# mLSTM's values ahead of stick breaking, and a start whose ACT and DVE order is written out

## The chip, the cores and the metric

The kernel runs on one core of one Trainium2 chip. The metric is the device time of one execution in microseconds (us), median of several runs; less is better. The engines of the core are TensorE (PE, matmuls), VectorE (DVE), ScalarE (ACT), GpSimd (POOL) and SyncE (SP, which starts most DMAs). Each engine runs its own list of instructions strictly in order; semaphores make one engine wait for another.

## The reference

Two layers of a hybrid block are applied to x (256 positions, width 1024), with 256 memory rows beside it. In each layer the normed x is projected to five branches of width 512 with 4 heads of 128, and to gates:

```
proj = rms_norm(x) @ w_in
y_sb = stick_breaking(sb_q, sb_k, sb_v)       # softplus, cumsum over keys, exp
y_ml = head_norm(mlstm(conv(ml_q), conv(ml_k), ml_v, i, f)) * sigmoid(ml_o)
y_gm = spatial_gating(gelu(gm_u), gelu(gm_v))
y_rt = head_norm(retention(rotary(rt_q), rotary(rt_k), rt_v))
y_xa = attention(xa_q, mem_k, mem_v)          # mem_k, mem_v = rms_norm(mem) @ w_mem_kv
merged = sum over branches b of sigmoid(gate_b) * ((y_b * silu(z_b)) @ w_up_b)
x = x + rms_norm(merged @ w_out)
```

Everything is fp32.

## The kernel before, in words

**Weights.** All weight matrices are cut into chunks of 128 x 2048, each of two halves of 128 x 1024, numbered in the order in which they are used (`CHUNKS`, from `SEQ_SECT`). SP loads a half into one of five `raw` buffers. ACT casts it to a rounded high part `whi` (L141), DVE subtracts to get the low part `wlo` (L142), and TensorE multiplies in three passes (high x high, low x high, high x low), which keeps fp32 accuracy. The input is kept in the same way as `hh` and `hl`. A half is 24 matmuls of 128 x 256 (`half_proj`, L216 to L218, output `psp`) or 12 of 128 x 512 (`half_nat`, L252 to L254, output `psn`), both eight blocks of the contraction, k0 to k7, by block order.

**A step.** `step(h)` splits half h+2, starts the load five halves on, issues the matmuls of half h, evacuates if a section ends, and pops a few units from `queue`. Units are the small pieces of the branches (scores, softplus, conv, gates, norms); so they lie between the halves.

**Order.** The whole program is traced in written order and then reordered by a scheduler with a model of the chip, engine by engine. Only inside `tc.manual_schedule(engines=...)` do the named engines keep the written order. In before this holds for SP in the prologue, for PE in the last matmuls of a layer and for SP, ACT, DVE and POOL in the tail.

**The prologue (layer 0).** The memory's keys (`mk`, halves 0 to 3) and values (`mv`, halves 4 to 7) are projected while x is loaded. Between them units do the memory's norm, the squares of x (L206), the product of x with its norm (`xr`, L378), the turning of x (`u2`, four times: four TensorE transposes into a PSUM tile `psh` that holds two blocks of x, then `hh` on ACT, L393, and `hl` on DVE, L394, block by block), and `rope_tables`: eight small DVE steps (`pf`, `ang`, `nn`) and then sin, abs and cos on ACT, which give `sinT` and `cosT`. mv is evacuated to a fp32 tile (L443) and split later by units (`mkv_split_units`, L449, L450). Half 8 is the first of `rt_q`, the first section of the layer, and needs `hh` and `hl`; half 12 is the first of `rt_v`.

**Stick breaking.** `sb_units` has three units for each of two head pairs g: `u1` (scores `psz`; abs, exp, ln on ACT, which are one softplus; a mask on POOL; high and low part `sh`, `sl`), `u2` (products of the triangle matrix with `sh` and `sl` into psz, exp to `sw`) and `u3` (values). Each change between exp and ln, and to tanh, needs a load of ACT's table. The units are popped during the section of mLSTM's values (`ml_v_section`, L725), which follows the four sb sections, and after it; `ml_gate_units` m1 to m4 (psc, psg, psm) are behind them.

Of the kernel before, what the change touches and what calls it, by code (L numbers as in the profile page):

```python
# [9 lines left out]
F32 = mybir.dt.float32  # L10
# [12 lines left out]
NSH = 1  # L23
# [8 lines left out]

SEQ_SECT = ["rt_q", "rt_v", "rt_k", "rt_z", "sb_q", "sb_k", "sb_v", "sb_z",
            "ml_v", "ml_q", "ml_k", "ml_z", "ml_o", "xa_q", "xa_z", "gm_u", "gm_v", "gm_z"]
BR = ["rt", "sb", "ml", "xa", "gm"]
# [48 lines left out]
def hybrid_kernel(ctx: ExitStack, tc: tile.TileContext, x, mem, wpl, wmv, pos, vec, row, post, gmw, cst, out):  # L84
# [325 lines left out]
    def mkv(l, units):  # L410
# [31 lines left out]
        def vevac(tb, ps):  # L442
            act.activation(mv[2][:, tb, :], ps, AF.Copy, scale=rcm[:, tb:tb + 1])  # L443
        nat(4, mh, ml, vevac, units)

    def mkv_split_units():

        def u(hi, lo, a):
            act.copy(hi, a)  # L449
            dve.tensor_tensor(lo, a, fview(hi), op=ALU.subtract)  # L450
        return [lambda m=m, s=s: u(*(a[:, s, :] for a in state[m]))
                for m, n in (("mk", 2), ("mv", 1)) for s in (slice(0, n), slice(n, 2 * n))]

    def layer(l):
# [84 lines left out]

        def sb_units():  # L540
            zp, sp, wt, po = {}, {}, {}, {}

            def part(tl, i):

                return (tl[:, 0:512] if i == 0 else tl[:, 512:768]).rearrange("p (h q) -> p h q", h=2)
# [7 lines left out]
            def u1(g):  # L553
                q, k = t["sb_q"], t["sb_k"]
                pss = [pz.tile([128, 2, 256 >> i], F32, tag="sm", name="psz") for i in range(2)]
                s = tp.tile([128, 768], F32, tag="sa", name="sa", bufs=2)
                hi = tp.tile([128, 768], F32R, tag="sh", name="sh", bufs=NSH)
                lo = tp.tile([128, 768], F32R, tag="sl", name="sl", bufs=NSH)
                for i in range(2):
                    for j in range(2):  # L560
                        h = 2 * g + j
                        pe.matmul(pss[i][:, j, :], k[:, h, i * 128:(i + 1) * 128], q[:, h, i * 128:T], start=j == 0,
                                  stop=False, skip_group_check=True)
                for i in range(2):
                    a = part(s[:], i)
                    act.activation(a, pss[i], AF.Abs)
                    act.activation(a, a, AF.Exp, scale=-1.0)
                    act.activation(a, a, AF.Ln, bias=1.0)
                    dve.scalar_tensor_tensor(a, pss[i], 0.0, a, op0=ALU.max, op1=ALU.add)
                mask(s[:])  # L570
                for c in (slice(0, 512), slice(512, 768)):
                    act.copy(hi[:, c], s[:, c])
                    dve.tensor_tensor(lo[:, c], s[:, c], fview(hi[:, c]), op=ALU.subtract)
                zp[g], sp[g] = pss, (hi, lo)

# [24 lines left out]

            return waves([[lambda g=g: u1(g), lambda g=g: u2(g), lambda g=g: u3(g)] for g in range(2)])

# [55 lines left out]
        def ml_gate_units():  # L658
            def m1():
                g = tp.tile([128, 2, 8], F32, tag="mg", name="mg", bufs=1)  # L660
                for tb in range(2):
                    dve.tensor_tensor(g[:, tb, :], psc["if"][tb], bif, op=ALU.add)
                f = g[:, :, 4:8]
                a = tp.tile([128, 2, 4], F32, tag="ma", name="ma", bufs=1)
                act.activation(a, f, AF.Abs)
                act.activation(a, a, AF.Exp, scale=-1.0)
                act.activation(a, a, AF.Ln, bias=1.0)
                lf = tp.tile([128, 2, 4], F32, tag="mlf", name="mlf", bufs=1)
                dve.scalar_tensor_tensor(lf, f, 0.0, a, op0=ALU.min, op1=ALU.subtract)
                t["g"], t["lf"] = g, lf  # L670

# [34 lines left out]

            return [m1, m2, m3, m4]

# [288 lines left out]
        queue.extend(mkv_split_units())  # L997
        nat(4, xh, xl, vcopy_to("rt_v"))
        section(proj, rope_to("rt_k"))
        nat(4, xh, xl, silu_nat("rt_z"))  # L1000
        drain()
        queue.extend(rt_units())
        section(proj, copy_to("sb_q", SCALE))
        section(proj, copy_to("sb_k"))
        nat(4, xh, xl, vcopy_to("sb_v"))
        section(proj, silu_to("sb_z"))
        drain()
        queue.extend(sb_units())
# [159 lines left out]
    with tc.manual_schedule(engines={mybir.EngineType.SP}):  # L1168
# [16 lines left out]
        for tb in range(2):  # L1185
# [114 lines left out]
```

## Time and profile before

| | |
|---|---|
| median of 3 runs | 919.64 us (919.44 to 919.68) |
| the profiled execution | 920.07 us |
| its span, first to last instruction | 918.2 us |
| mean granted TensorE clock | 0.998 |
| DVE busy | 603.7 us (66%) |
| ACT busy | 488.4 us (53%) |
| HBM read | 161.8 MB, 177 GB/s over the span |

The span is the profiled execution's stretch from its first to its last instruction; 1.9 us of the 920.07 lie around it. A matmul's record is longer than the distance to the next, since matmuls are pipelined: distances between starts tell what one costs. The granted clock is a share of TensorE's full speed of 2.4 GHz.

### The profile page before, as it was taken

The page shows a single profiled execution, that of the slowest core. Times are in us where ns is not written, and L with a number is a line of the kernel's source. Part 1 is how long each engine was busy: PE and PEld are TensorE (multiplying, and loading weights), DVE is VectorE, ACT ScalarE, POOL GpSimd, SP SyncE. Part 2 cuts the span into 40 slices and gives each one's busy share as a digit, 9 for nine tenths or more (in the row PEclk, how much of TensorE's full clock was granted, in tenths as well). Part 3 has the DMA queues.
Part 4 walks back from the last instruction along what each step waited for, and adds up shares of the span by engine and source line. Part 5 has one row for each costly group of instructions (what it writes and reads, how often), then busy time and mean ns, then how long its engine had stood idle before and what let it go on. Part 6 is the DMA issues. An engine that isn't in the chain of part 4 may idle for free.

```text
span 918.2 us, 13638 instructions
## 1 busy us (share of the span) xinstructions
PE 905.6 (99%) x5332; PEld 798.5 (87%) x5332; DVE 603.7 (66%) x882; ACT 488.4 (53%) x682; POOL 46.2 (5%) x66
## 2 busy tenths in 40 slices
PE   9999999999999999999999999999999999999997
PEld 7899999989998888888899999998999888888885
DVE  6776565776685665765588656559667765665555
ACT  6645459654665444455465444686556554444443
POOL 1000001000040000000010000010011300000000
PEclk9999999999999999999999999999999999999999
DMA  9665453554445545555556544435444545455551
GB/s 336 247 206 180 144 184 116 178 180 148 161 166 179 184 164 194 190 178 191 206 184 227 186 162 164 173 124 177 167 161 159 179 167 181 166 194 193 188 201 46
DMA packets 45857, 163.74 MB, mean 178 GB/s; under 512 B 5216, under 2 KB 5344, under 8 KB 45792
## 3 DMA queue, kind: packets, MB, share of 16 engines
q1 hardware_dynamic: 45072, 161.56, 49.8%
q10 hardware_dynamic: 720, 1.32, 0.4%
q8 instruction: 41, 0.67, 0.3%
q14 instruction: 24, 0.20, 0.1%
HBM read 161.80 MB, written 1.05 MB: 177 GB/s over the span
## 4 chain that ended last, share of the span: by engine, by line
PE 92%; ACT 2%; DMA 2%; issue 1%; DVE 1%; POOL 0%; ACTq 0%; DVEq 0%; POOLq 0%; SPq 0%
PE psn L252 17%; PE psn L253 17%; PE psn L254 17%; PE psp L218 9%; PE psp L217 9%; PE psp L216 9%; PE pout L1082 1%; PE pout L1084 1%; PE pout L1083 1%; DMA xn<-in_x_dram 1%; DMA memT<-in_mem_dram 1%; PE pss L766 1%; PE psx L877 1%; PE pso L911 1%; DVE wlo L142 1%
## 5 line engine op out<-in xcount | busy, mean ns | idle before, releaser
L142 DVE TENSOR_TENSOR wlo<-raw,whi 128x1024 fp32r<-128x1024 f32 (+1 forms) x293 | 359.8, 1230 | 229.7 <-ACT whi L141 228.7
L141 ACT CAST whi<-raw 128x1024 fp32r<-128x1024 f32 (+1 forms) x293 | 307.0, 1049 | 335.8 <-PE psn L254 185.1
L253 PE MATMUL psn<-wlo,hh 128*128 128x512 f32 x512 | 202.8, 396 | 0.0
L216 PE MATMUL psp<-hh,whi 128*128 128x256 f32 x704 | 200.5, 285 | 0.8 <-ACT whi L141 0.8
L254 PE MATMUL psn<-whi,hl 128*128 128x512 f32 x512 | 201.2, 393 | 0.0
L218 PE MATMUL psp<-hh,wlo 128*128 128x256 f32 x704 | 199.7, 284 | 0.5 <-DVE wlo L142 0.5
L217 PE MATMUL psp<-hl,whi 128*128 128x256 f32 x704 | 198.4, 282 | 0.0
L252 PE MATMUL psn<-whi,hh 128*128 128x512 f32 x512 | 185.9, 394 | 0.0
L216 PEld LDWEIGHTS psp<-hh,whi 128*128 128x128 f32 x704 | 133.1, 189 | 1.7 <-ACT whi L141 1.0
L218 PEld LDWEIGHTS psp<-hh,wlo 128*128 128x128 f32 x704 | 133.0, 189 | 1.0 <-DVE wlo L142 0.7
L217 PEld LDWEIGHTS psp<-hl,whi 128*128 128x128 f32 x704 | 132.9, 189 | 0.6
L254 PEld LDWEIGHTS psn<-whi,hl 128*128 128x128 f32 x512 | 96.2, 188 | 20.3
L253 PEld LDWEIGHTS psn<-wlo,hh 128*128 128x128 f32 x512 | 96.2, 188 | 20.1
L252 PEld LDWEIGHTS psn<-whi,hh 128*128 128x128 f32 x512 | 95.4, 188 | 20.9
L253 PE MATMUL psn<-wlo,yh 128*128 128x512 f32 x160 | 63.4, 396 | 0.0
L254 PE MATMUL psn<-whi,yl 128*128 128x512 f32 x160 | 62.6, 391 | 0.0
L252 PE MATMUL psn<-whi,yh 128*128 128x512 f32 x160 | 56.7, 393 | 0.0
L252 PEld LDWEIGHTS psn<-whi,yh 128*128 128x128 f32 x160 | 30.0, 188 | 6.9
L253 PEld LDWEIGHTS psn<-wlo,yh 128*128 128x128 f32 x160 | 30.1, 188 | 6.5
L254 PEld LDWEIGHTS psn<-whi,yl 128*128 128x128 f32 x160 | 30.1, 188 | 6.3
L1048 ACT ACTIVATE gate<-psn 128x512 f32<-128x512 f32 x40 | 24.0, 599 | 20.1 <-PE psn L254 20.1
L1083 PE MATMUL pout<-wlo,mgh 128*128 128x512 f32 x64 | 24.6, 395 | 0.0
(287 smaller groups left out, 1015.4 us busy)
## 6 DMA issues: line engine op xcount, KB each, us to landing
raw<-in_wpl_dram SPq DMA_DIRECT2D x290, 512.0 KB, 3.4
raw<-in_wmv_dram SPq DMA_DIRECT2D x4, 528.0 KB, 4.3
rowb<-in_row_dram SPq DMA_DIRECT2D x2, 772.0 KB, 7.3
raw<-in_wpl_dram SPq DMA_DIRECT2D x4, 256.0 KB, 6.2
xn<-in_x_dram SPq DMA_DIRECT2D x2, 512.0 KB, 7.6
gpost<-in_post_dram SPq DMA_DIRECT2D x2, 512.0 KB, 5.8
memT<-in_mem_dram ACTq DMA_DIRECT2D x3, 256.0 KB, 7.2
cs<-in_cst_dram SPq DMA_DIRECT2D x1, 768.0 KB, 7.1
```

The source lines that it names most:

```text
L141: act.copy(hi[:, c], r[:, c])
L142: dve.tensor_tensor(lo[:, c], r[:, c], fview(hi[:, c]), op=ALU.subtract)
L216: pe.matmul(ps_ap, wh(k), xh(k), start=st, stop=False, skip_group_check=True)
L217: pe.matmul(ps_ap, wh(k), xl(k), start=False, stop=False, skip_group_check=True)
L218: pe.matmul(ps_ap, wl(k), xh(k), start=False, stop=last and k == nk - 1, skip_group_check=True)
L252: pe.matmul(pss[tb], a, hi[:, c], start=k == 0, stop=False)
L253: pe.matmul(pss[tb], a, lo[:, c], start=False, stop=False)
L254: pe.matmul(pss[tb], b, hi[:, c], start=False, stop=k == 2 * nq - 1)
L766: pe.matmul(ps[:, 0:256], k[:, h, 0:128], q[:, h, :], start=True, stop=False, skip_group_check=True)
L877: pe.matmul(ps[:, tb, :], q[i], k[j], start=tb == 0 and i == j, stop=tb == 1 and i == 1, skip_group_check=True)
L1048: nat(4, xh, xl, lambda tb, ps: act.activation(gt[:, tb, :], ps, AF.Tanh, scale=0.5))
L1083: pe.matmul(po[tb][i], a, lo[:, c], start=False, stop=False)
```

## The change

1. `ml_v` moves ahead of the sb sections, in the order of chunks and in the program. Its matmuls, loads and splits go there.
2. `sb_units` takes the gate units as an argument. `u1` does both abs, both exp, both ln; the cast and subtract to `sh`, `sl` are a unit `us` of their own. The order becomes u1(0), u1(1) (with m0 and m1 of the gates inside it, split so that their exp and ln stand beside sb's), us(0), u2(0) with m2, us(1) with m3, u2(1) with m4, u3(0), u3(1).
3. mv is evacuated straight to its high part (ACT) and its low part (DVE, out of PSUM); the fp32 tile and two of four split units go.
4. From `mkv(0, ...)` until after rt_v of layer 0, ACT and DVE join SP in the manual region and keep the written order. The numbers of units popped in the prologue become 1, 2, 3, 2, 2, 1.
5. The first two of the four units that turn x stand ahead of `rope_tables`, the last two behind it.

```
-SEQ_SECT = ["rt_q", "rt_v", "rt_k", "rt_z", "sb_q", "sb_k", "sb_v", "sb_z",
-            "ml_v", "ml_q", "ml_k", "ml_z", "ml_o", "xa_q", "xa_z", "gm_u", "gm_v", "gm_z"]
+SEQ_SECT = ["rt_q", "rt_v", "rt_k", "rt_z", "ml_v", "sb_q", "sb_k", "sb_v", "sb_z",
+            "ml_q", "ml_k", "ml_z", "ml_o", "xa_q", "xa_z", "gm_u", "gm_v", "gm_z"]
...
         def vevac(tb, ps):
-            act.activation(mv[2][:, tb, :], ps, AF.Copy, scale=rcm[:, tb:tb + 1])
+            act.activation(mv[0][:, tb, :], ps, AF.Copy, scale=rcm[:, tb:tb + 1])
+            dve.scalar_tensor_tensor(mv[1][:, tb, :], ps, rcm[:, tb:tb + 1], fview(mv[0][:, tb, :]), op0=ALU.mult,
+                                     op1=ALU.subtract)
...
         return [lambda m=m, s=s: u(*(a[:, s, :] for a in state[m]))
-                for m, n in (("mk", 2), ("mv", 1)) for s in (slice(0, n), slice(n, 2 * n))]
+        return [lambda s=s: u(*(a[:, s, :] for a in state["mk"])) for s in (slice(0, 2), slice(2, 4))]
...
+                a = [part(s[:], i) for i in range(2)]
                 for i in range(2):
-                    a = part(s[:], i)
-                    act.activation(a, pss[i], AF.Abs)
-                    act.activation(a, a, AF.Exp, scale=-1.0)
-                    act.activation(a, a, AF.Ln, bias=1.0)
-                    dve.scalar_tensor_tensor(a, pss[i], 0.0, a, op0=ALU.max, op1=ALU.add)
+                    act.activation(a[i], pss[i], AF.Abs)
+                for i in range(2):
+                    act.activation(a[i], a[i], AF.Exp, scale=-1.0)
+                if g == 1:
+                    gate[0]()
+                for i in range(2):
+                    act.activation(a[i], a[i], AF.Ln, bias=1.0)
+                    dve.scalar_tensor_tensor(a[i], pss[i], 0.0, a[i], op0=ALU.max, op1=ALU.add)
+                if g == 1:
+                    gate[1]()
                 mask(s[:])
+                zp[g], sp[g] = pss, s
+
+            def us(g):
+                s = sp[g]
+                hi = tp.tile([128, 768], F32R, tag="sh", name="sh", bufs=NSH)
+                lo = tp.tile([128, 768], F32R, tag="sl", name="sl", bufs=NSH)
                 for c in (slice(0, 512), slice(512, 768)):
                     act.copy(hi[:, c], s[:, c])
                     dve.tensor_tensor(lo[:, c], s[:, c], fview(hi[:, c]), op=ALU.subtract)
-                zp[g], sp[g] = pss, (hi, lo)
+                sp[g] = hi, lo
...
-            return waves([[lambda g=g: u1(g), lambda g=g: u2(g), lambda g=g: u3(g)] for g in range(2)])
+            return [lambda: u1(0), lambda: u1(1), lambda: us(0), both(lambda: u2(0), gate[2]),
+                    both(lambda: us(1), gate[3]), both(lambda: u2(1), gate[4]), lambda: u3(0), lambda: u3(1)]
...
         nat(4, xh, xl, vcopy_to("rt_v"))
+        if l == 0:
+            state.pop("region").close()
...
         queue.extend(rt_units())
+        ml_v_section()
         section(proj, copy_to("sb_q", SCALE))
...
         drain()
-        queue.extend(sb_units())
-        ml_v_section()
-        queue.extend(ml_gate_units())
+        queue.extend(sb_units(ml_gate_units()))
...
-        queue.extend(xu[:2] + [mem_cols, lambda: [f() for f in state.pop("mk_evac")]] + xu[2:3] +
-                     [lambda: rope_tables(state.pop("pos"))] + xu[3:])
-        mkv(0, [1, 1, 2, 1, 3, 3])
+        queue.extend(xu[:2] + [mem_cols, lambda: [f() for f in state.pop("mk_evac")]] + xu[2:5] +
+                     [lambda: rope_tables(state.pop("pos"))] + xu[5:])
+        region = state["region"] = ExitStack()
+        E = mybir.EngineType
+        region.enter_context(tc.manual_schedule(engines={E.SP, E.Activation, E.DVE}))
+        mkv(0, [1, 2, 3, 2, 2, 1])
```

**The start on ACT.** First before, from the cast of half 5 (whi_215) to that of half 8 (whi_310):

```order
L141 CAST whi_215<-raw_175 128x1024 [waits DMAHW0_49]
L141 CAST whi_258<-raw_177 128x1024 [waits DMAHW1_49,DVE_49,PE_49]
L326 ACT_TABLE_LOAD
L326 ACTIVATE sinT_81<-ang_332 128x256 [waits DVE_49]
L199 COPY rbm_82<-psb_286 128x256 [waits PE_49]
L327 ACTIVATE ang_332<-ang_332 128x256 [waits Activation_49]
L141 CAST whi_290<-raw_213 128x1024 [waits DMAHW4_49]
L393 ACTIVATE hh_328<-psh_347,vecs_77 128x256 [waits DMAHW2_49,PE_49]
L330 ACTIVATE cosT_80<-ang_332,hp_344 128x256 [waits Activation_49]
L449 CAST mkh_152<-mk_156 128x512 [waits DVE_49] x2
L141 CAST whi_310<-raw_183 128x1024 [waits DMAHW2_49,PE_49]
```

The change, from the fourth block of hh to the two evacuations of mv; whi_331 is half 8, whi_375 half 9:

```order
L393 ACTIVATE hh_293<-psh_322,vecs_77 128x256 [waits DVE_49]
L141 CAST whi_331<-raw_184 128x1024 [waits DMAHW2_49,Activation_49]
L310 CAST tri_r_79<-cs_76 128x256
L326 ACT_TABLE_LOAD
L326 ACTIVATE sinT_81<-ang_351 128x256 [waits DVE_49]
L327 ACTIVATE ang_351<-ang_351 128x256 [waits Activation_49]
L330 ACTIVATE cosT_80<-ang_351,hp_363 128x256 [waits DVE_49,Activation_49]
L393 ACTIVATE hh_293<-psh_366,vecs_77 128x256 [waits PE_49]
L393 ACTIVATE hh_293<-psh_366,vecs_77 128x256 [waits DVE_49]
L141 CAST whi_375<-raw_191 128x1024 [waits DMAHW3_49,PE_49]
L442 ACTIVATE mvh_156<-psn_267,rcm_83 128x512 [waits PE_49,Pool_49]
L442 ACTIVATE mvh_156<-psn_268,rcm_83 128x512 [waits PE_49]
```

The sine table's load, sin and abs stood between the casts of halves 6 and 7, and cos behind the first hh; now all of them stand behind four blocks of hh and the cast of half 8, and ahead of the fifth block of hh.

**The start on DVE.** Before, from the first x product to the last step that gives ang and what follows it:

```order
L378 TENSOR_SCALAR xr_254<-xn_78,n0y_252 128x1024 [waits DMAHW5_49,Pool_49]
L314 TENSOR_SCALAR ang_332<-pf_330,cs_76 128x256 [waits DMAHW4_49,DVE_49]
L208 SCALAR_TENSOR_TENSOR rv_281<-ss_276 128x1 [waits Activation_49]
L192 TENSOR_SCALAR nv_210<-psn_207 128x2 [waits PE_49]
L317 TENSOR_SCALAR nn_333<-ang_332 128x256 [waits DVE_49]
L318 TENSOR_SCALAR nn_333<-nn_333 128x256 [waits DVE_49]
L378 TENSOR_SCALAR xr_254<-xn_78,n1y_283 128x1024 [waits DMAHW6_49,Pool_49]
L323 SCALAR_TENSOR_TENSOR ang_332<-nn_333,ang_332 128x256 [waits DVE_49]
L142 TENSOR_TENSOR wlo_216<-raw_175,whi_215 128x1024 [waits DMAHW0_49,Activation_49]
L323 SCALAR_TENSOR_TENSOR ang_332<-nn_333,ang_332 128x256 [waits DVE_49] x2
L142 TENSOR_TENSOR wlo_259<-raw_177,whi_258 128x1024 [waits DMAHW1_49,PE_49,Activation_49]
L325 TENSOR_SCALAR ang_332<-ang_332 128x256 [waits DVE_49]
```

The change, from the third and fourth block of hl to the first mv pass:

```order
L394 SCALAR_TENSOR_TENSOR hl_294<-psh_322,vecs_77,hh_293 128x256 [waits Activation_49] x2
L142 TENSOR_TENSOR wlo_332<-raw_184,whi_331 128x1024 [waits DMAHW2_49,DVE_49,Activation_49]
L313 CAST pf_349<-posb_120 128x256 [waits DMAHW7_49]
L314 TENSOR_SCALAR ang_351<-pf_349,cs_76 128x256 [waits DVE_49]
L317 TENSOR_SCALAR nn_352<-ang_351 128x256 [waits DVE_49]
L318 TENSOR_SCALAR nn_352<-nn_352 128x256 [waits DVE_49]
L323 SCALAR_TENSOR_TENSOR ang_351<-nn_352,ang_351 128x256 [waits DVE_49] x3
L325 TENSOR_SCALAR ang_351<-ang_351 128x256 [waits DVE_49]
L329 MEMSET hp_363 128x1
L394 SCALAR_TENSOR_TENSOR hl_294<-psh_366,vecs_77,hh_293 128x256 [waits Activation_49] x2
L142 TENSOR_TENSOR wlo_376<-raw_191,whi_375 128x1024 [waits DMAHW3_49,Activation_49]
L443 SCALAR_TENSOR_TENSOR mvl_157<-psn_267,rcm_83,mvh_156 128x512 [waits Activation_49]
```

The rotary steps stood between the x products and the subtracts of halves 5 and 6; now they stand in one piece behind the subtract of half 8 (wlo_332) and ahead of the last four blocks of hl.

**The first section on PE.** Before, from the fourth block of half 8 (whi_310, psp_410) on; psp_479 with whi_411 is half 10:

```order
L216 MATMUL psp_410<-hh_328,whi_310 128x256 [waits Activation_49]
L217 MATMUL psp_410<-hl_329,whi_310 128x256 [waits DVE_49]
L218 MATMUL psp_410<-hh_328,wlo_311 128x256
L216 MATMUL psp_479<-hh_328,whi_411 128x256 [waits Activation_49]
L217 MATMUL psp_479<-hl_329,whi_411 128x256
L216 MATMUL psp_410<-hh_328,whi_310 128x256 [waits Activation_49]
L218 MATMUL psp_479<-hh_328,wlo_412 128x256 [waits DVE_49]
L216 MATMUL psp_479<-hh_328,whi_411 128x256
L217 MATMUL psp_479<-hl_329,whi_411 128x256
```

The change, around the same blocks of half 8 (whi_331, psp_413):

```order
L216 MATMUL psp_413<-hh_293,whi_331 128x256
L217 MATMUL psp_413<-hl_294,whi_331 128x256
L218 MATMUL psp_413<-hh_293,wlo_332 128x256
L216 MATMUL psp_413<-hh_293,whi_331 128x256 [waits Activation_49]
L217 MATMUL psp_413<-hl_294,whi_331 128x256 [waits DVE_49]
L218 MATMUL psp_413<-hh_293,wlo_332 128x256
L216 MATMUL psp_413<-hh_293,whi_331 128x256 [waits Activation_49]
L217 MATMUL psp_413<-hl_294,whi_331 128x256 [waits DVE_49]
L218 MATMUL psp_413<-hh_293,wlo_332 128x256
```

Blocks of half 10 stood between the blocks of half 8; now half 8 is in the order of its blocks, with a wait for hh and one for hl at each of the last four.

**Stick breaking on ACT, layer 0.** Before, around u1 of the second head pair (sa_1532, sh_1533):

```order
L566 ACTIVATE sa_1532<-psz_1530 128x512 [waits PE_49,Activation_49]
L666 ACTIVATE ma_1717<-ma_1717 128x8 [waits Activation_49]
L567 ACTIVATE sa_1532<-sa_1532 128x512 [waits Activation_49]
L667 ACT_TABLE_LOAD
L667 ACTIVATE ma_1717<-ma_1717 128x8 [waits Activation_49]
L568 ACTIVATE sa_1532<-sa_1532 128x512 [waits Activation_49]
L566 ACTIVATE sa_1532<-psz_1531 128x256 [waits PE_49]
L141 CAST whi_1643<-raw_1407 128x1024 [waits DMAHW5_49,PE_49]
L567 ACT_TABLE_LOAD
L567 ACTIVATE sa_1532<-sa_1532 128x256 [waits Activation_49]
L572 CAST sh_1533<-sa_1532 128x512 [waits Pool_49]
L568 ACT_TABLE_LOAD
```

The change, u1 of the second pair (sa_1614) and the piece of the first that is still open (sa_1566, sh_1669):

```order
L564 ACTIVATE sa_1566<-psz_1565 128x256 [waits PE_49]
L566 ACTIVATE sa_1566<-sa_1566 128x256 [waits Activation_49]
L570 ACT_TABLE_LOAD
L570 ACTIVATE sa_1566<-sa_1566 128x256 [waits Activation_49]
L141 CAST whi_1639<-raw_1438 128x1024 [waits DMAHW6_49,DVE_49,PE_49]
L755 COPY ml_q_1531<-psp_1533 128x2x256 [waits PE_49]
L582 CAST sh_1669<-sa_1566 128x256 [waits Pool_49]
L564 ACTIVATE sa_1614<-psz_1612 128x512 [waits PE_49]
L564 ACTIVATE sa_1614<-psz_1613 128x256 [waits PE_49]
L566 ACT_TABLE_LOAD
L566 ACTIVATE sa_1614<-sa_1614 128x512 [waits Activation_49]
L566 ACTIVATE sa_1614<-sa_1614 128x256 [waits Activation_49]
```

ml_v's evacuations are gone from this place; the second pair's exp and ln stand in two blocks with one table load each, and its sh (sh_1758) follows later, behind two weight casts.

## Rows read from the trace of the kernel before

**Rows 1.** The page, part 1: busy us (share of the span) and instructions.

```profile
PE 905.6 (99%) x5332; PEld 798.5 (87%) x5332; DVE 603.7 (66%) x882; ACT 488.4 (53%) x682; POOL 46.2 (5%) x66
```

**Rows 2.** Waits of PE: line, waited for: us in total, times, longest.

```profile
PE psz L581 <- ACT sh L572: 3.0, 2, 1.5
```

**Rows 3.** Timeline of PE, 150 to 156.5 us: start, us, operation, idle before.

```profile
153.76 0.28 PE L216 MATMUL psp<-hh,whi 128*128 128x256 f32 x1
155.55 0.51 PE L581 MATMUL psz<-sh,tri_r 128*128 128x512 f32 x1 [1.51 <-ACT sh L572]
```

**Rows 4.** Timeline of PE, 31.5 to 37.2 us.

```profile
32.57 0.82 PE L389 MATMUL psh<-cs,xr 128*128 128x128 f32 x6
33.15 0.36 PE L216 MATMUL psp<-hh,whi 128*128 128x256 f32 x1
...
33.58 0.29 PE L216 MATMUL psp<-hh,whi 128*128 128x256 f32 x1
...
34.53 0.28 PE L218 MATMUL psp<-hh,wlo 128*128 128x256 f32 x1
35.63 0.39 PE L216 MATMUL psp<-hh,whi 128*128 128x256 f32 x1 [0.82 <-ACT whi L141]
```

**Rows 5.** Timeline of PE, 46.2 to 47.2 us.

```profile
46.65 0.63 PE L252 MATMUL psn<-whi,hh 128*128 128x512 f32 x2
```

**Rows 6.** Groups of ACT, 13 to 47 us: count, busy us, mean ns, idle before.

```profile
L141 ACT CAST whi<-raw 128x1024 fp32r<-128x1024 f32 x12 | 12.5, 1048 | 7.9 <-PE psp L217 5.6 <-DMA raw<-in_wpl_dram 2.3
...
L443 ACT ACTIVATE mv<-psn,rcm 128x512 f32<-128x512 f32 x2 | 1.4, 692 | 0.1
...
L330 ACT ACTIVATE cosT<-ang,hp 128x256 f32<-128x256 f32 x1 | 0.5, 506 | 0.0
```

**Rows 7.** Groups of DVE, 13 to 47 us.

```profile
L142 DVE TENSOR_TENSOR wlo<-raw,whi 128x1024 fp32r<-128x1024 f32 x10 | 12.2, 1222 | 3.9 <-ACT whi L141 3.9
L394 DVE SCALAR_TENSOR_TENSOR hl<-psh,vecs,hh 128x256 fp32r<-128x256 f32 x8 | 3.7, 477 | 0.5 <-ACT hh L393 0.5
...
L418 DVE TENSOR_TENSOR mk<-psk,rbm 128x512 f32<-128x512 f32 x2 | 1.3, 686 | 0.7 <-ACT rbm L199 0.7
...
L323 DVE SCALAR_TENSOR_TENSOR ang<-nn,ang 128x256 f32<-128x256 f32 x3 | 1.3, 421 | 0.0
```

**Rows 8.** Timeline of ACT, 13 to 39 us.

```profile
16.58 0.63 ACT L206 ACTIVATE sq<-xn 128x512 f32<-128x512 f32 x1 [0.76 <-DMA xn<-in_x_dram]
...
19.52 1.06 ACT L141 CAST whi<-raw 128x1024 fp32r<-128x1024 f32 x1 [0.30 <-DMA raw<-in_wpl_dram]
...
25.17 0.42 ACT L326 ACTIVATE sinT<-ang 128x256 f32<-128x256 f32 x1 [1.93 <-DVE ang L325]
...
33.07 0.47 ACT L393 ACTIVATE hh<-psh,vecs 128x256 fp32r<-128x256 f32 x1 [0.69 <-DVE hl L394]
```

**Rows 9.** Timeline of DVE, 17 to 28 us.

```profile
18.24 0.29 DVE L313 CAST pf<-posb 128x256 f32<-128x256 int32 x1
...
27.14 1.23 DVE L142 TENSOR_TENSOR wlo<-raw,whi 128x1024 fp32r<-128x1024 f32 x1
```

**Rows 10.** Stretches of 2 us: busy of PE, PEld, DVE, ACT, POOL, PEclk, DMA, GB/s.

```profile
912.00:914.00 2.00, 0.00 (x0) 0.00 (x0) 1.39 (x3) 0.51 (x2) 0.56 (x1) 1.00 0.38 148
914.00:916.00 2.00, 0.00 (x0) 0.00 (x0) 0.79 (x2) 0.00 (x0) 0.00 (x0) 0.51 0.48 185
```

**Rows 11.** Timeline of PE, 910.8 to 914 us.

```profile
911.33 0.40 PE L1084 MATMUL pout<-whi,mgl 128*128 128x512 f32 x1
```

**Rows 12.** Timeline of PE, 0 to 8 us.

```profile
1.34 4.63 PE L1175 MATMUL pw<-wm 128*128 128x256 f32 x10 [1.34 <-POOL wm L1172]
6.40 1.78 PE L296 MATMUL psk<-mg,raw 128*128 128x256 f32 x7 [0.43 <-DVE mg L350]
```

**Rows 13.** Timeline of ACT, 145 to 166 us.

```profile
150.03 1.28 ACT L667 ACT_TABLE_LOAD   x1
151.32 0.21 ACT L667 ACTIVATE ma<-ma 128x8 f32<-128x8 f32 x1
```

More of the change, by code (lines that the diff above doesn't have):

```diff
@@ L415, in mkv @@
         mk.append(bp.tile([128, H, T], F32, tag="gate", name="mk", bufs=2))
-        mv.append(bp.tile([128, 2, W], F32, tag="gate", name="mv", bufs=2))
         def evac(c, ps):
@@ L450, in u @@
             dve.tensor_tensor(lo, a, fview(hi), op=ALU.subtract)
-        return [lambda m=m, s=s: u(*(a[:, s, :] for a in state[m]))
-                for m, n in (("mk", 2), ("mv", 1)) for s in (slice(0, n), slice(n, 2 * n))]
+        return [lambda s=s: u(*(a[:, s, :] for a in state["mk"])) for s in (slice(0, 2), slice(2, 4))]
     def layer(l):
@@ L537, in diag, with sb_units @@
             return tl.rearrange("p (b q) -> p b q", b=3)[:, 0:3:2, :]
-        def sb_units():
+        def sb_units(gate):
             zp, sp, wt, po = {}, {}, {}, {}
@@ L556, in u1 @@
                 s = tp.tile([128, 768], F32, tag="sa", name="sa", bufs=2)
-                hi = tp.tile([128, 768], F32R, tag="sh", name="sh", bufs=NSH)
-                lo = tp.tile([128, 768], F32R, tag="sl", name="sl", bufs=NSH)
                 for i in range(2):
@@ L599, in u3, with both @@
                 y_from("sb", po, t["sb_z"], g)
-            return waves([[lambda g=g: u1(g), lambda g=g: u2(g), lambda g=g: u3(g)] for g in range(2)])
+            def both(*f):
+                return lambda: [u() for u in f]
+            return [lambda: u1(0), lambda: u1(1), lambda: us(0), both(lambda: u2(0), gate[2]),
+                    both(lambda: us(1), gate[3]), both(lambda: u2(1), gate[4]), lambda: u3(0), lambda: u3(1)]
         def waves(chains):
@@ L658, in ml_gate_units, with m0 @@
         def ml_gate_units():
-            def m1():
+            def m0():
                 g = tp.tile([128, 2, 8], F32, tag="mg", name="mg", bufs=1)
@@ L666, in m1 @@
                 act.activation(a, a, AF.Exp, scale=-1.0)
+                t["g"], t["ga"] = g, a
+            def m1():
+                g, a = t["g"], t["ga"]
+                f = g[:, :, 4:8]
                 act.activation(a, a, AF.Ln, bias=1.0)
@@ L669, in m1 @@
                 dve.scalar_tensor_tensor(lf, f, 0.0, a, op0=ALU.min, op1=ALU.subtract)
-                t["g"], t["lf"] = g, lf
+                t["lf"] = lf
             def m2():
@@ L705, in m4 @@
                 t["em"] = em
-            return [m1, m2, m3, m4]
+            return [m0, m1, m2, m3, m4]
         def ml_v_section():
```

## The prediction

> **What bounds the kernel now.** I read the page first: TensorE is busy for 905.6 of 918.2 us [rows 1], so only time in which it stands still, or runs at its lower clock, can be won or lost. The waits of PE say which those are: apart from the first microseconds the largest is psz behind sh, twice, 3.0 us in all [rows 2]. The timeline of PE around the first of them shows what one costs: the matmul ahead starts at 153.76 and psz at 155.55, where 0.12 is the usual distance, so 1.67 us, once in each layer, 3.3 us together [rows 3]. The other loss lies in the prologue. rt_q of layer 0 runs from 33.15 to the first psn of rt_v at 46.65, 13.5 us [rows 4, 5]; its 96 matmuls at the distance of [rows 4] (33.58 to 34.53, eight of them, 0.119 each) need 11.4, so 2.1 us are waits, the longest 0.82 for the cast of half 10. Nearly everything else is back to back. So the change is judged at two places: the two psz waits can give 3.3, rt_q's waits 2.1; all else can only cost.
>
> **The prologue, as now written.** ACT and DVE run what their order says, one after the other. Durations: cast 1.05, mv's evacuation 0.69, cos 0.51 [rows 6]; subtract 1.22, hl 0.48, a 128x512 pass out of PSUM 0.69, a rotary step on two tensors 0.42 [rows 7], one on a single tensor 0.29, by pf [rows 9]; hh 0.47, sin 0.42, and I take the same for abs, which has its shape [rows 8]. ACT overlaps two neighbours by some 0.1, a dependent step begins about 0.04 after its source.
>
> Early part: the squares of x, from 16.58 in before, now stand behind the cast of half 5, which waits for its DMA until 19.5 [rows 8]. They end some 3.6 later, and so do the x products on DVE. The cover is TensorE's work on mv, which lasts until 32.7; the first hh still comes at about 27.0, so I cost this at nothing. If the cover were gone it would cost up to 3.6.
>
> Turning x: hh of block k+1 waits for hl of block k where both lie in one PSUM tile; before shows it as hh with 0.69 idle behind hl [rows 8]. DVE had finished the subtract of half 7 at 27.14 + 1.23 = 28.4 [rows 9]; with the second x product and both mk products ahead of it I take 28.7. From there hl0, hh1, hl1, hl2, hh3, hl3 follow as a chain to 31.6. The cast of half 8 stands behind hh3 on ACT (to 32.0), its subtract behind hl3 on DVE (to 33.3).
>
> Then the rotary tables. Before started them at 18.24 in the gaps of DVE, and sin ran at 25.17 [rows 8, 9]. Now all eight DVE steps stand behind the subtract of half 8: five of 0.29 and three of 0.42 with 0.04 between are 3.0 us, to 36.2. ACT has loaded the sine table by then and waits: sin, abs, cos, to 37.7. Queued behind cos on ACT is hh of k4, and behind that everything: hh4 is there at 38.05.
>
> TensorE is ahead of this. It issues the last mv matmul and reaches rt_q at 32.7 (the last six transposes, from 32.57 in before [rows 4], now lie earlier), waits 0.34 for the subtract of half 8, and has done k0 to k3 at 34.5. In the new PE order half 8 runs strictly from k0 to k7, where before put half 10's first blocks in between. So it waits 3.6 for hh4. Then k4 and k5 cost 1.07 (hl4, hh5, hl5, one after the other). Ahead of hh6 ACT does the cast of half 9 and both mv evacuations (to 41.2), so hh6 costs 1.74; ahead of hl6 DVE does that half's subtract and the two new mv passes (to 42.5), so hl6 costs 1.21; hh7 and hl7 0.67. Sum 0.34 + 3.60 + 1.07 + 1.74 + 1.21 + 0.67 = 8.6. rt_v starts at 32.7 + 11.4 + 8.6 = 52.7 in place of 46.65 [rows 5]: **+6.1 us**. TensorE has no slack later to give it back.
>
> **The clock.** After the last matmul (911.33, 0.40 long) the granted clock is 0.51 in the stretch 914 to 916: it went from 2.4 to 1.2 GHz some 2.3 us after that matmul ended [rows 10, 11]. The wait for hh4 has 3.3 us without a matmul, and the next 5 us have few. At the program's start the ten pw matmuls, 0.46 apart, take 4.63 us, and the same kind runs 0.25 apart from 6.40 [rows 12], so some 4.6 us of work pass at the lower clock before it rises, which costs half of them. Here the dense work resumes at 43.9. I add **2.3**; ends 0 (no fall, or full speed again by 44) and 4.0 (full speed only with rt_v, at 52: half of the 8 us from 44). The Trainium skill, page "TensorE: Matmul & The Clock Gate", Part 1, calls the throttled clock the default to which an idle engine returns; by it the 2.3 is paid, and the row at the end agrees.
>
> **Values straight from PSUM.** mv's fp32 tile and its two split units go: two casts and two subtracts less, two DVE passes out of PSUM more, which I price by mk's 0.69 [rows 7]. They are counted above. No DMA is added; the weight loads keep their number, ml_v's chunks stand earlier on SP's queue because the section does. That queue runs five halves ahead throughout (five raw buffers), so the move costs nothing; without that cover TensorE would stand for what a load is late.
>
> **The stick-breaking stage, per layer.** Before put ml_v between sb_z and ml_q, and the sh of the second head pair came 1.67 after TensorE wanted it. Now u1(0) starts inside sb_z, us(0) is a unit of its own, and u2(0) stands 72 matmuls (8.6 us) and four psz behind the last psz of pair 0, while ACT needs about 6 us for what lies ahead of sh (abs, exp, a table load, ln, a cast, one copy, sh). u2(1) stands 96 matmuls behind its psz, 11.4 us and the psz besides, against about 10 on ACT. So both waits go: **-3.3**. What is late next is psc: its PSUM buffer is free only when ACT has read sw, and by the same walk that comes within 0.1 of TensorE's arrival; 0 taken, 0.5 a layer as the upper end. The cast of the last sb_z half, behind ACT's abs, load, exp, load, ln of pair 0, has 0.65 to spare: no cost, up to 0.5 a layer. ACT's table loads go from 6 to 8 a layer here; at 1.28 each and with the next ACTIVATE 0.01 behind [rows 13] they lie in the walk. The Trainium skill, page "ScalarE: Activation LUTs", section "What ACT_TABLE_LOAD costs", adds a drain of about 1.38 us to every switch. By that page the three loads ahead of psc would make it 4.1 later in each layer and the sum 933 (an estimate from its figure); [rows 13] show no drain.
>
> **Sum.** The profiled execution took 920.07 (span 918.2), 0.43 above the runs' median of 919.64. 920.07 + 6.1 + 2.3 - 3.3 = 925.2; on the runs' scale **924.7**.
>
> **The rivals.**
> *The clock holds.* 922.4. For it: the only fall that the trace shows is one, at the end, and half 8's few matmuls break up the idle time. Against it: 3.3 us without any matmul is more than the 2.3 after which it fell. Chance 0.20.
> *The stage gains less or nothing.* If the two extra loads and the cast ahead of sb_z put waits of 0.5 to 1.7 a layer in place of the old, the time is 925.7 to 928. For it: the margins of 0.1 and 0.65. Chance 0.09.
> *Each table switch holds ACT longer than its load.* If it were twice the 1.28, the three loads between u1(1) and psc would bring psc 3.8 late in each layer: 924.7 + 7.7 = 932.4. Against it: the next ACTIVATE starts 0.01 behind the load [rows 13]. Chance 0.01.
> *Faster: the start's chain is shorter than the stage's gain.* One mechanism: the chain hl0 to hl7, with the rotary steps in it. If it ends before 40.8 instead of 43.9, rt_v starts less than 3.1 us late, the wait for hh4 is too short for the clock, and the 3.3 of the two stages win; with the chain hidden altogether (rt_v at 46.65) it is 919.64 - 3.3 = 916.3, with rt_q's 2.1 gone too 914.2. For it: the stage's gain is sure by comparison. Against it: eight DVE steps, three on ACT and the two mv passes must then lie elsewhere, and the written order leaves them no other place. Chance 0.08.
> *The change does not do what it says* (the start's order is as free as before): 916.3 as well; the new order of both engines says otherwise, 0.02 within the last.
>
> **How the numbers follow.** Forecast 924.7, chance 0.62 with its own range 923.5 to 926.5; the clock case 0.20, the stage case 0.09, the table case 0.01, the faster case 0.08. About 0.2%, or 1.8 us, is what a measurement of this kernel can tell from no change, so the same is 917.8 to 921.5. Faster by more: 0.06, most of the last case. Same: 0.08, the rest of it and the lower part of the clock case with a start that loses 1 less. Slower: 0.86. The range leaves out the faster case and the worst of the stage case: 921.2 to 927.0.
>
> **What would show it.** In the profile after: rt_v's first psn near 52.7; a PE wait of over 3 us for hh near 34.6, led by ACT's cos; psp behind hl and hh a few times more before 44; a granted clock below 1 somewhere from 36 to 48, and matmuls of 128x256 more than 0.2 apart there; no psz behind sh in either layer; eight table loads there. The prediction is wrong if rt_v starts before 50, if the order of half 8's blocks on PE hides hh4, or if PE shows new waits over 1 us at psc or at sb_z's last half.

## The result, and the profile after

The changed kernel takes 925.16 us (median of 4 runs, 924.10 to 925.97), before 919.66 (4 runs); the ratio is 1.0055, 95% interval 1.004 to 1.007. It is slower, by 5.5 us, where 924.7 was forecast. The profiled execution took 924.86 with a span of 923.1, 4.9 more than before's 918.2, and a mean granted clock of 0.992.

The waits of PE, line and what was waited for, us in total, times, longest. The two psz waits of [rows 2] are gone; hh and hl have come:

```profile
PE psp L216 <- ACT hh L393: 4.5, 2, 3.3
PE pw L1195 <- POOL wm L1192: 1.3, 1, 1.3
PE psp L217 <- DVE hl L394: 0.9, 1, 0.9
```

The timeline of PE around rt_q, the counterpart of [rows 4, 5] (start, us, operation, idle before):

```profile
33.59 0.28 PE L216 MATMUL psp<-hh,whi 128*128 128x256 f32 x1
...
34.92 0.28 PE L218 MATMUL psp<-hh,wlo 128*128 128x256 f32 x1
38.51 0.58 PE L216 MATMUL psp<-hh,whi 128*128 128x256 f32 x1 [3.30 <-ACT hh L393]
...
42.00 0.58 PE L216 MATMUL psp<-hh,whi 128*128 128x256 f32 x1 [1.15 <-ACT hh L393]
43.44 0.58 PE L217 MATMUL psp<-hl,whi 128*128 128x256 f32 x1 [0.86 <-DVE hl L394]
...
48.04 0.40 PE L218 MATMUL psp<-hh,wlo 128*128 128x256 f32 x1
...
48.40 0.28 PE L217 MATMUL psp<-hl,whi 128*128 128x256 f32 x1
...
55.06 0.63 PE L252 MATMUL psn<-whi,hh 128*128 128x512 f32 x2
```

rt_q starts at 33.59 and rt_v at 55.06, where before had 33.15 and 46.65: 8.4 us late. The last matmul of block k3 stands at 34.92, the first of k4 at 38.51; k6 waits again for its hh (42.00) and its hl (43.44). The timeline of ACT in the same stretch:

```profile
36.69 0.42 ACT L326 ACTIVATE sinT<-ang 128x256 f32<-128x256 f32 x1 [2.64 <-DVE hp L329]
37.14 0.42 ACT L327 ACTIVATE ang<-ang 128x256 f32<-128x256 f32 x1
37.58 0.51 ACT L330 ACTIVATE cosT<-ang,hp 128x256 f32<-128x256 f32 x1
38.00 0.46 ACT L393 ACTIVATE hh<-psh,vecs 128x256 fp32r<-128x256 f32 x1
...
40.31 1.27 ACT L442 ACTIVATE mvh<-psn,rcm 128x512 fp32r<-128x512 f32 x2
41.46 0.48 ACT L393 ACTIVATE hh<-psh,vecs 128x256 fp32r<-128x256 f32 x1
```

And the timeline of DVE:

```profile
24.97 0.75 DVE L378 TENSOR_SCALAR xr<-xn,n1y 128x1024 f32<-128x1024 f32 x1 [0.66 <-POOL n1y L102]
...
27.97 1.22 DVE L142 TENSOR_TENSOR wlo<-raw,whi 128x1024 fp32r<-128x1024 f32 x1
29.11 0.47 DVE L394 SCALAR_TENSOR_TENSOR hl<-psh,vecs,hh 128x256 fp32r<-128x256 f32 x1
...
32.48 1.23 DVE L142 TENSOR_TENSOR wlo<-raw,whi 128x1024 fp32r<-128x1024 f32 x1 [0.45 <-ACT whi L141]
33.62 0.29 DVE L313 CAST pf<-posb 128x256 f32<-128x256 int32 x1
...
36.36 0.29 DVE L325 TENSOR_SCALAR ang<-ang 128x256 f32<-128x256 f32 x1
...
41.59 1.40 DVE L443 SCALAR_TENSOR_TENSOR mvl<-psn,rcm,mvh 128x512 fp32r<-128x512 f32 x2
42.91 0.47 DVE L394 SCALAR_TENSOR_TENSOR hl<-psh,vecs,hh 128x256 fp32r<-128x256 f32 x1
```

The second x product starts at 24.97, the subtract of half 7 at 27.97, and the first hl, with which the chain of hh and hl begins, at 29.11. The subtract of half 8 starts at 32.48, the first rotary step at 33.62, the last at 36.36; ACT has been idle for 2.64 when sin starts at 36.69; then come cos and, at 38.00, hh of k4. Behind that mv's two evacuations stand ahead of hh of k6 on ACT (40.31, 41.46), mv's two passes ahead of its hl on DVE (41.59, 42.91).

The stretches of 2 us (busy of PE, PEld, DVE, ACT, POOL, then PEclk, DMA share, GB/s):

```profile
36.00:38.00 2.00, 0.00 (x0) 0.00 (x0) 0.62 (x3) 1.25 (x4) 0.00 (x0) 1.00 0.18 70
38.00:40.00 2.00, 1.49 (x4) 1.08 (x4) 0.97 (x2) 1.45 (x4) 0.00 (x0) 0.51 0.00 0
...
46.00:48.00 2.00, 2.00 (x11) 2.00 (x11) 1.31 (x2) 0.12 (x1) 0.00 (x0) 0.50 0.99 404
48.00:50.00 2.00, 2.00 (x18) 2.00 (x17) 0.44 (x1) 0.52 (x1) 0.00 (x0) 0.93 0.96 350
```

From 38 to 48 the granted clock is 0.50, which is 1.2 GHz; up to 48.04 the matmuls start 0.21 apart, from 48.40 on 0.12. TensorE started no matmul between 34.92 and 38.51.

Later, the stage. The group of PE from 130 to 180 us that waited in before:

```profile
L591 PE MATMUL psz<-sh,tri_r 128*128 128x512 f32 x2 | 0.8, 390 | 0.0
```

And the timeline of ACT at the first pair's exp and ln:

```profile
142.82 1.28 ACT L566 ACT_TABLE_LOAD   x1
144.11 0.63 ACT L566 ACTIVATE sa<-sa 128x512 f32<-128x512 f32 x1
144.76 1.28 ACT L570 ACT_TABLE_LOAD   x1
146.06 0.63 ACT L570 ACTIVATE sa<-sa 128x512 f32<-128x512 f32 x1
```

psz behind sh no longer has any idle time ahead of it, against 1.5 in before [rows 3]. Each table load of 1.28 is followed by its ACTIVATE 0.01 to 0.02 later, as in [rows 13].

Not everything in this stage stands where the program writes it, since the scheduler orders ACT freely there. The gates' m0 and m1, written inside u1(1), run at 103.90 and 105.44 with a table load of their own between them. And not every change to or from tanh takes a load: behind the load for tanh at 149.52 an exp at 156.67 runs without one.

The account: rt_v is 8.41 later, the two psz waits (1.67 and, in layer 1, 1.65) are 3.32 less, which makes 5.09; the last matmul starts 4.94 later than in before [rows 11]:

```profile
916.27 0.40 PE L1104 MATMUL pout<-whi,mgl 128*128 128x512 f32 x1
```

### The profile page after: what moved, and what is told of

Read it like the earlier page. It is cut to its first block, busy times and chain, and to the rows that moved or that the text cites. A ratio compares the mean times of both kernels' runs of the same rounds, so it can differ in the third digit from the quotient of the medians.

```text
span 923.1 us, 13648 instructions
## 1 busy us (share of the span) xinstructions
PE 909.8 (99%) x5332; PEld 802.3 (87%) x5332; DVE 606.6 (66%) x882; ACT 488.6 (53%) x678; POOL 45.5 (5%) x66
## 3 DMA queue, kind: packets, MB, share of 16 engines
q10 hardware_dynamic: 720, 1.32, 0.4%
## 4 chain that ended last, share of the span: by engine, by line
PE 95%; DVE 2%; DMA 1%; issue 1%; ACT 1%; DVEq 0%; POOLq 0%; POOL 0%; ACTq 0%
PE psn L252 17%; PE psn L253 17%; PE psn L254 17%; PE psp L217 9%; PE psp L216 9%; PE psp L218 9%; PE pout L1102 1%; PE pout L1104 1%; PE pout L1103 1%; DMA raw<-in_wpl_dram 1%; PE psk L296 1%; PE pss L785 1%; PE psx L896 1%; PE pso L930 1%; PE psz L560 1%
## 5 line engine op out<-in xcount | busy, mean ns | idle before, releaser
L142 DVE TENSOR_TENSOR wlo<-raw,whi 128x1024 fp32r<-128x1024 f32 x293 | 360.1, 1232 | 231.6 <-ACT whi L141 230.4
L141 ACT CAST whi<-raw 128x1024 fp32r<-128x1024 f32 x293 | 306.6, 1048 | 335.0 <-PE psn L254 187.3
L216 PE MATMUL psp<-hh,whi 128*128 128x256 f32 x704 | 202.6, 288 | 4.5 <-ACT hh L393 4.5
```

The source lines that it names most:

```text
L141: act.copy(hi[:, c], r[:, c])
L142: dve.tensor_tensor(lo[:, c], r[:, c], fview(hi[:, c]), op=ALU.subtract)
L216: pe.matmul(ps_ap, wh(k), xh(k), start=st, stop=False, skip_group_check=True)
```

## The experiments

Nine kernels were run, one of them twice: four on one chip, then three on a second and three on a third, each group beside before (919.66, 919.70 and 919.84 us). The theory is the prediction's: the start loses through the rotary tables' place and mv's evacuation ahead of hh, the low clock comes on top, and the stage gains its two waits.

### e1: the stage alone

Parts 1 and 2 of the change, on before's prologue:

```
-        queue.extend(... + xu[2:5] + [lambda: rope_tables(state.pop("pos"))] + xu[5:])
-        region.enter_context(tc.manual_schedule(engines={E.SP, E.Activation, E.DVE}))
-        mkv(0, [1, 2, 3, 2, 2, 1])
+        queue.extend(... + xu[2:3] + [lambda: rope_tables(state.pop("pos"))] + xu[3:])
+        mkv(0, [1, 1, 2, 1, 3, 3])
```

and mv's evacuation and split as in before.

> The change's parts 1 and 2 alone (ml_v ahead of stick breaking, the units of stick breaking and of the gates in their new order); the prologue and the evacuation of mv are those of before. My theory: the two psz waits of 1.67 go, nothing comes in their place, so 919.66 - 3.3 = 916.3 us. Rival that the start's delay itself made room in the later stages: the psz waits come back or psc waits, 917.5 or more. Rival that the new order also loses elsewhere: 919 or more.

916.43 us, ratio 0.9964 (0.9949 to 0.9978): 3.2 less than before. The waits of PE hold no psz and no psc; what is left behind the first microseconds are rt_q's two:

```profile
PE psp L216 <- ACT whi L141: 1.0, 1, 1.0
PE psp L218 <- DVE wlo L142: 0.5, 1, 0.5
```

The gain does not hang on the start's delay, and the new order of the stage takes nothing back.

### e2: the start alone

Parts 3 to 5 on before's stages (the reverse of e1's edit).

> Parts 3 to 5 alone (mv straight from PSUM, ACT and DVE in written order until after rt_v, x turned ahead of the rotary tables); the stages from rt_k on are those of before. My theory: rt_v starts 8.4 later than in before, as in the changed kernel, and both psz waits stay: 919.66 + 8.4 = 928.1 us. Rival that part of the 8.4 is given back later: below 926.5.

928.84 us, ratio 1.010 (1.0085 to 1.0115): 9.2 more than before. Both groups of waits stand side by side:

```profile
PE psp L216 <- ACT hh L393: 4.4, 2, 3.3
PE psz L581 <- ACT sh L572: 3.0, 2, 1.5
```

e1's 3.2 less and e2's 9.2 more make 5.9, the changed kernel has 5.5 more: the parts add up, within the spread of the runs. In e2's profile rt_v starts at 54.48 and the last matmul at 919.16, both 7.83 later than in before: nothing of the start's loss is given back later. The profiled execution is 8.7 longer than before's, so some 0.8 of that lies behind the last matmul, where the change does nothing; why, no run shows.

### e3: the changed kernel with a free order

```
-        E = mybir.EngineType
-        region.enter_context(tc.manual_schedule(engines={E.SP, E.Activation, E.DVE}))
         mkv(0, [1, 2, 3, 2, 2, 1])
```

> The changed kernel, but ACT and DVE are free to be reordered in the prologue, as in before; units, the place of the rotary tables in the program and mv's evacuation are the change's. Theory that the written order is what costs: the rotary steps lie early again, rt_v starts at 46 to 46.7, the time is 915.0 to 916.3 us. Rival that turning x ahead of the rotary tables, or the new pop numbers, cost by themselves: rt_v at 50 or later, 920 us or more.

915.47 us, ratio 0.9953 (0.9938 to 0.9968); run again as e10 it took 915.71. The scheduler puts the rotary steps where before had them, though the program writes them behind the turns of x. Its timeline of DVE, the first and the last of the steps:

```profile
18.59 0.29 DVE L313 CAST pf<-posb 128x256 f32<-128x256 int32 x1 [0.95 <-DMA posb<-in_pos_dram]
...
24.67 0.29 DVE L325 TENSOR_SCALAR ang<-ang 128x256 f32<-128x256 f32 x1
```

Its timeline of PE, the start of rt_q, its one wait and the start of rt_v:

```profile
32.96 0.36 PE L216 MATMUL psp<-hh,whi 128*128 128x256 f32 x1
...
36.14 0.39 PE L218 MATMUL psp<-hh,wlo 128*128 128x256 f32 x1 [0.82 <-DVE wlo L142]
...
45.55 0.63 PE L252 MATMUL psn<-whi,hh 128*128 128x512 f32 x2
```

pf at 18.59, the last step at 24.67, and rt_v at 45.55, 9.5 us ahead of the changed kernel, with one wait of 0.82 in rt_q. So neither the pop numbers nor the written place of the rotary tables cost anything while the order is free; holding ACT and DVE to what is written does. Which piece of it costs what, e5 and e6 show.

### e4: TensorE's long waits filled

Half 8 gets 45 more matmuls into a tile that nobody reads:

```
+                if k == 6:
+                    dummy(6, 8)
...
+                if k in (3, 5):
+                    dummy(k, 27 if k == 3 else 10)
```

> The changed kernel with 45 more matmuls of 128x256 in half 8 of rt_q, into a PSUM tile that nobody reads: 27 behind k3, 10 in k5 and 8 in k6, each lot shorter than TensorE's wait there. Theory that the lower clock from 38 to 48 is a cost of its own, of 2.4 us: the clock stays at 1.00, the waits for hh and hl keep their ends (38.5, 42.0, 43.4), rt_v starts at 52.7 and the time is 922.7 us. Rival that the low clock is covered by the waits: the time stays at 925.2. Rival that the filler delays the blocks behind it: 926 or more.

922.92 us, ratio 1.0031 (1.0018 to 1.0044): 2.24 less than the changed kernel, with 45 matmuls more. Its stretches of 2 us, and the start of rt_v on PE:

```profile
38.00:40.00 2.00, 1.86 (x11) 1.46 (x12) 1.01 (x3) 1.53 (x3) 0.00 (x0) 1.00 0.00 0
...
46.00:48.00 2.00, 2.00 (x19) 2.00 (x19) 1.35 (x3) 0.74 (x1) 0.00 (x0) 1.00 1.04 408
```

```profile
52.84 0.63 PE L271 MATMUL psn<-whi,hh 128*128 128x512 f32 x2
```

The clock stays at 1.00 and rt_v starts at 52.84 in place of 55.06. rt_q itself started at 33.04, 0.55 earlier than in the changed kernel's profile, so of the 2.22 some 1.7 are the clock's in this pair of profiles. The lower clock is a cost of its own; the rest of the start's loss stays in e4.

### e5: the rotary tables written early

The written order stays; the eight DVE steps go, in pieces, ahead of the memory norm and around the two x products, and sin, abs and cos ahead of the first hh:

```
+        ra, rb, rc, rd = rope_units(state.pop("pos"))
+        queue.insert(0, ra)
+        xu = x_norm_units(0, (rb, rc))
+        queue.extend(xu[:2] + [mem_cols, lambda: [f() for f in state.pop("mk_evac")]] + xu[2:3] + [rd] + xu[3:])
...
+        mkv(0, [2, 2, 3, 3, 1, 1])
```

> The changed kernel, ACT and DVE still in written order, with the rotary tables written early: the DVE steps in four pieces ahead of the memory norm's column and around the two x products, sin, abs and cos behind the cast of half 7 and ahead of the first hh. Everything else is the change's. Theory that the place of the rotary tables is what costs most, and not that the order is written: the wait for hh4 goes, the clock stays at 1.00, the waits for hh6, hl6 and hl7 behind mv's evacuation stay (about 3.4 in all): 918.7 us. Rival that any written order costs what this one does, since the hh and hl pairs follow one another: 923 or more.

921.66 us (919.87 to 922.54, 11 runs), ratio 1.0019 (1.001 to 1.0028): 3.5 better than the changed kernel, 3.0 worse than expected. The wait for hh of k4 is gone, as expected. Two things were missed. In its profile cos waits for a fill of 0.06 us on DVE that was written behind the subtract of half 7 (timelines of ACT and, below, of DVE):

```profile
29.41 0.51 ACT L341 ACTIVATE cosT<-ang,hp 128x256 f32<-128x256 f32 x1 [1.29 <-DVE hp L340]
```

```profile
28.07 1.22 DVE L142 TENSOR_TENSOR wlo<-raw,whi 128x1024 fp32r<-128x1024 f32 x1
29.24 0.06 DVE L340 MEMSET hp<- 128x1 f32 x1
```

and the clock fell (0.62 from 40 to 42 us, mean 0.997), though no wait in rt_q was longer than 1.22; e9 takes that up.

### e6: x turned in pairs of tiles, ahead of mv

e5, and hh of one tile, hh of the other, hl, hl, with the second pair ahead of mv's evacuation:

```
+            for j in range(2):
+                for m, ps in enumerate(pss):
+                    k = 4 * i + 2 * m + j
...
+        mkv(0, [2, 2, 3, 2, 1, 0])
```

> The same, and x turned in pairs of PSUM tiles (hh of one tile, hh of the other, then hl, hl) and wholly ahead of mv's evacuation. Theory that the rest of the loss is the chain of single pairs and mv's two passes ahead of hh6 and hl6: no wait over 0.5 in rt_q, rt_v starts at 45.2 to 45.6, the time is 915.1 us, as good as the free order. Rival that the later x products delay the subtract of half 6 and TensorE waits there instead: 916.5 or more.

915.85 us, ratio 0.9959 (0.9946 to 0.9973): 5.8 less than e5, with the same early rotary tables, and 0.75 more than expected. In its profile rt_v starts at 45.89, and two waits for a low part are left in rt_q, of 0.50 and 0.38. Between e5 and e6 stand the single pairs and mv ahead of hh of k6; they cost 5.8 together, with the clock that falls with them, and no run takes them apart. A written order is not dear as such: e5's step of 3.5 and this one lead from the changed kernel to within 0.4 of the free order.

### e7: the stage, and mv straight from PSUM

e1 with part 3.

> The stage alone (parts 1 and 2) with mv straight from PSUM (part 3), in a free order and with the units and the place of the rotary tables of before. Theory that part 3 is the source of the free order's extra 1.0 against the stage alone: 915.5 us. Rival that turning x ahead of the rotary tables gives it: 916.4 us.

916.07 us, ratio 0.9959 (0.9946 to 0.9971), between the two values expected: by the times this is undecided. The waits of PE speak for part 3: e1's wait of 1.0 for the cast of half 10 is not among them, the 0.5 for its subtract is.

```profile
PE psp L218 <- DVE wlo L142: 0.5, 1, 0.5
```

### e8, e9, e10: two small steps moved, and e3 again

In e6 (as e8) and e5 (as e9):

```
         def a():
+            dve.memset(hp, float(np.float32(np.pi / 2)))
+            act.copy(tri_r, cs[:, C_TRIN:C_TRIN + 256])
             dve.tensor_copy(pf, posb)
```

with both lines taken from where sin and cos are issued.

> e6 with two small steps moved: the fill of the bias column hp goes to the head of the rotary steps on DVE (in e6 it stood behind the subtract of half 7, and cos waited for it), and the cast of the triangle matrix goes to ACT's wait for half 5. Theory that hp set the start of the hh chain: cos ends near 28.6, the first hh comes near 28.7 in place of about 30, the two waits for wlo in rt_q (1.2 together) go, 914.7 us. Rival that the chain hangs on the subtract of half 7 anyway: no more than 0.3 better than e6, 915.6.

914.86 us, ratio 0.9942 (0.9928 to 0.9955). The waits of PE hold nothing of rt_q any more, only the first microseconds:

```profile
PE pw L1227 <- POOL wm L1224: 1.3, 1, 1.3
PE psk L296 <- DVE mg L364: 0.5, 1, 0.5
```

Its profiled execution, 916.48, is the slowest of the five: TensorE was 1.7 late from the first ten microseconds on (last section), the cast of half 7 started at 26.18 behind a late rbm, and the first hh came at 29.86, not at 28.7. So the trace does not show what hp cost. The median is 1.0 below e6's, where 1.15 was expected; e6 ran on another chip, and which of the two steps gave how much is not taken apart.

> e5 with the same two steps moved. Theory: the waits of 0.8 and 0.9 at the head of rt_q go, the waits behind mv's evacuation stay (about 3 in all); if the clock holds, 918.0 us, if it falls again (as in e5, where TensorE worked little from 33 to 41 without one long gap), 919.5 to 920.5. Rival that e5's 921.7 did not come from the head of rt_q: 921 or more.

920.94 us (918.39 to 922.09, 11 runs), ratio 1.0007 (0.9998 to 1.0016). In the profiled execution, 922.09, the raw data of half 7 landed late, so the waits at the head of rt_q stayed (0.3 and 0.8). The median is 0.4 above what was expected of a clock that falls and just short of the rival's 921, so the times leave open what the head of rt_q cost. As expected, the waits behind mv's evacuation are 1.20 and 1.06, and the clock falls behind them (timeline of PE, then stretches of 2 us):

```profile
38.49 0.39 PE L216 MATMUL psp<-hh,whi 128*128 128x256 f32 x1 [1.20 <-ACT hh L409]
39.94 0.39 PE L217 MATMUL psp<-hl,whi 128*128 128x256 f32 x1 [1.06 <-DVE hl L410]
```

```profile
38.00:40.00 2.00, 0.45 (x2) 0.25 (x2) 1.88 (x4) 0.53 (x3) 0.00 (x0) 1.00 0.42 141
40.00:42.00 2.00, 1.86 (x11) 1.46 (x12) 1.12 (x2) 1.90 (x3) 0.00 (x0) 1.00 0.97 334
42.00:44.00 2.00, 2.00 (x12) 2.00 (x11) 1.73 (x2) 0.47 (x1) 0.00 (x0) 0.52 1.03 413
```

Of its eleven executions the one of 918.39 has a mean clock of 0.999, as was expected of a clock that holds (918.0); the others have 0.994 to 0.997 and 919.57 to 922.09.

> The kernel of e3 once more, beside e8 on one chip. Theory that a written order can be as good as the free one: 915.5 us, and e8 below it by 0.5 to 1. Rival that the free order stays ahead: e8 above 915.5.

915.71 us, ratio 0.9951 (0.9939 to 0.9964). e8 is 0.85 below it at the median on the same chip. Four of e8's five runs lie at 914.73 to 914.99, all of e10's at 915.12 to 916.29; e8's fifth, 916.48, is its profiled one. So a written order can be as good as the free one, and e8 has the lowest median of all: 5.0 us less than before, where the changed kernel is 5.5 more.

## Why the prediction was right

The sum was 6.1 + 2.3 - 3.3. Measured term by term:

**The stage, -3.3.** Right: -3.2 by e1, both waits gone, no wait at psc and none at sb_z's last half. The rival that the two extra table loads would bring new waits is out, and so is the one in which a load holds ACT longer than it lasts. The forecast's 6 and 8 loads a layer hold for this stage alone: over the whole kernel both profiles have 23 loads, since a later stage has two fewer a layer, which the prediction did not see. The drain that the Trainium skill, page "ScalarE: Activation LUTs", section "What ACT_TABLE_LOAD costs", adds to a switch shows in no row here: the next ACTIVATE came 0.01 to 0.02 behind each load shown, and the sum by that page, 933, is 8 too high.

**The clock, 2.3.** Right in kind, and too large by 0.1 to 0.6. It fell within the wait for hh of k4, as the prediction had it. By the medians e4 gives 2.2; by the length of rt_q in the two profiles 21.47 - 19.80 = 1.7, since e4's rt_q also began 0.55 earlier. The clock came back at 48.2, 3.1 us after the dense work resumed at 45.05, where the sum had reckoned with 4.6. The rival in which the clock holds is out.

**The waits of rt_q, 6.1.** Right in kind and place. Of rt_q's 21.47 us, 11.4 are matmuls and 1.7 the clock, so 8.4 are waits, 8.6 forecast: 3.47 for hh of k4 (3.60 forecast), 1.45 for hh of k6 (1.74), 1.32 for its hl (1.21), the rest in small ones. One step is plainly wrong: "reaches rt_q at 32.7 (the last six transposes now lie earlier)". Transposes that lie earlier are still TensorE's work, so moving them gives nothing; rt_q began at 33.59, 0.44 later than in before instead of 0.45 earlier, 0.3 of it from the first microseconds. For the same reason the wait of 0.34 for the subtract of half 8 did not come. This error cost no time, since TensorE has to wait for hh of k4 in either case. What sets rt_v is the end of the chain of hh and hl, and that was late from its first link on.

**The early part, 0.** Wrong, by little. The squares of x began at 20.52 where before had 16.58 [rows 8], and the second x product at 24.97 where before had 20.78. TensorE did have other work until 33.59, but DVE had no such cover: the subtract of half 6, both mk products and the subtract of half 7 stand behind the second x product and run without a break. So the subtract of half 7 began at 27.97 (27.14 in before [rows 9]) and the first hl at 29.11, though its hh was there at 28.20. The prediction had allowed for 28.7, and its times stay 0.4 behind from there on: the subtract of half 8 ended at 33.71 (33.3 forecast), cos at 38.09 (37.7), hh of k4 at 38.46 (38.05). By this trace the late squares are worth up to 0.9 (29.11 less 28.2, an estimate); no run moves them alone.

**The sum.** Half 8 ended at 45.05, where the prediction's terms put it at 44.2 (32.7 + 8.6 and 24 matmuls), 0.9 late. From there the 72 matmuls to rt_v took 10.0 us, 1.4 more than at full speed (the rest of the clock's 1.7 lies in half 8), where 2.3 had been added, 0.9 too much. The two errors cancel: rt_v came 8.4 later, and 6.1 + 2.3 is 8.4. The mechanism was right; that the number is this close is luck.

The rival in which the stage's gain wins over the start is out: 3.2 (e1) against 9.2 (e2). With the rotary tables out of the way (e5, e9), the waits behind mv's evacuation are the largest that remain, beside smaller ones at the head of rt_q.

## What to carry to other kernels

Where two engines are made to keep a written order, every unit in it has to be put where its engine would otherwise stand idle, down to a fill of 0.06 us for which cos waited 1.29 us (e5); a side chain that nobody needs yet (here the rotary tables) must not stand ahead of work that the bound engine is about to want. A wait on a matmul-bound path is to be priced with what the clock takes after it, and e4 is a quick way to tell the two apart: fill the wait with work that nobody reads. When a change has several parts, run the parts: here one part was worth 3.2 us and hidden under a loss of 9.

## What the runs showed of the hardware

Two things were not expected. The clock fell in e5 and e9 without any long gap: in e9's profile no wait in rt_q passes 1.20, yet it falls at 42, after ten microseconds in which TensorE was busy for 1.70, 1.24, 1.29, 0.45 and 1.86 of each 2 us. And it does not fall in every execution of the same program: of e9's eleven the one with a mean clock of 0.999 took 918.39 us and the others, with 0.994 to 0.997, took 919.57 to 922.09; of e5's eleven the one with 0.999 is the fastest too, at 919.87. Only one execution of each has a trace, so for the others this is read from the mean clock.

The column of the granted clock reads 1.00 in the first microseconds of every profile, also where matmuls of pw start 0.43 apart and, later, psk's of the same shape 0.22 apart. In e8's profiled execution psk went on at 0.43 until 10.1 us, in before's it ran at 0.22 from its start at 6.40; the difference is about 1.7 us, and that execution is 1.6 above e8's median. The distances between matmuls tell what that column does not.
